# An encoder layer on one core: the order of VectorE and ScalarE in attention written out, pv copied whole by ScalarE, its halves added by GpSimd, and o stored in two parts

## The chip, the core and the metric

The kernel runs on one core of one Trainium2 chip. The metric is device time in microseconds: the median of several executions. "The profiled execution" is one of them, taken with the hardware profiler; all durations of single instructions come from it. In the profile PE is TensorE (PEld its weight loads), DVE VectorE, ACT ScalarE, POOL GpSimd and SP SyncE; a q behind a name is that engine's instruction queue.

## The reference, cut to what matters

One layer with two token mixers over 1024 prompt frames and 64 frames of a running stream (1088 columns together). The part that the change touches is the band attention, and the gates and merge behind it:

```python
s = einsum('bqhd,bkhd->bhqk', q, k) * HEAD_DIM ** -0.5
s = where(allowed, s + bias, NEG_INF)   # own chunk of 64 and the 8 chunks before
p = softmax(s)
o = einsum('bhqk,bkhd->bqhd', p, v)     # 8 heads of 64
yb = o @ w_attn_out
merged = sigmoid(ga) * ya + sigmoid(gb) * yb
```

Ahead of it stand a norm and the combined input projection; behind it an output projection, a gated feed-forward part and two norms. All is 32-bit; the kernel gets its precision by splitting each operand into a rounded high part (hi) and the rest (lo), and taking products of the parts.

## The kernel before

**Attention** is a list of 72 tiles: 8 heads, and in each 9 tiles t (eight of 128 prompt frames, t = 0 to 7; t = 8 is the 64 frames of the stream with its cache). A loop in `attention` (line 974 on) walks over this list in steps, and a step i does the following for tiles at different distances:

- `scores` of tile i: the S products (q times k) into a PSUM bank of kind "att"; then `softmax`: VectorE adds the bias and takes the maximum (L856), ScalarE takes the exp with its row sums (L866);
- `transposed` of tile i - 2: TensorE turns p into a PSUM bank "att" (T, L774); then `split`: ScalarE casts it to hi (L122), VectorE subtracts to get lo (L123);
- `values` of tile i - 4, for odd t (two tiles together) and t = 8: the pv products into the one bank "pv". With hi and lo of v as 128 weight columns, pv has two halves of 64 rows, and hi and lo of p make two halves of its columns. `combine` adds all: ScalarE copies the lower 64 rows (L872), VectorE adds the upper 64 (L873), GpSimd adds the two column halves (L874), and SP's queue stores the result into o_d (L877, L881). For t = 8, the reciprocals of the row sums are turned too, copied by ScalarE (L949) and stored by GpSimd's queue in four parts (L951, L955).
- between these, `gate` hands out products of the gates ga and gb (32 pieces of 24 products; 5 run before attention, 16 in it, 11 after). A finished piece lies in the bank "mm" during attention, ScalarE copies it out (L792) and GpSimd's queue stores it (L793). After a piece is finished, the next call of `gate` gives nothing.

The banks are "att" 3, "mm" 1, "pv" 1. TensorE's order is the program's: `mm_at` and `turned` pin each product and turn. The order on ScalarE, VectorE, GpSimd and in SP's queue is set at compile time by a planner that takes, among the instructions that its own clock holds ready, the first of the program.

`head_load` (from line 822) loads q, k, bias and v of a head through SP's queue one head ahead; q, k, v have two buffers, the stream's keys and values (ks, vs) one.

**The merge** (from line 1014): SP's queue loads the gates of the first block (L1002), u (L1017), and for each quarter k of the 512 rows of o the rows of o_d (L1020) and the reciprocal sums, spread over 64 rows a head (L1024, tile rc with two buffers). VectorE multiplies (L1027), and `split` makes the hi and lo parts ob. Then the last gate pieces are handed out, and block by block TensorE takes ya (from u) and yb (from ob), L302, and VectorE multiplies each with its gate (L1043, L1048).

Of the kernel before, what the change touches and what calls it, by code (L numbers as in the profile page):

```python
# [65 lines left out]
def encoder_kernel(ctx: ExitStack, tc: tile.TileContext, ins, outs):  # L66
# [701 lines left out]
    mm0, turned0 = nc.tensor.matmul, nc.tensor.transpose  # L768

    def mm_at(*a, **kw):  # L770
        tc.keep_in_program_order(mm0(*a, **kw))  # L771

    def turned(*a):
        tc.keep_in_program_order(turned0(*a))  # L774

    def gates():

        kinds = itertools.chain(["att"] * (4 * len(GATES) - WITH - BEHIND), ["mm"] * WITH, turns)
        pieces = [(i, c) for cs in ((0, 1), (2, 3)) for i in range(2) for c in cs]
        pieces += [(i, c) for i in range(2, len(GATES)) for c in range(4)]  # L780
        w = {}
        for i, c in pieces:
            g, m = GATES[i]
            o, n = PIECES[c]
            if i not in w:
                w[i] = next_w()
# [5 lines left out]
            act.copy(st[:, :n], ps[:, :n])  # L792
            nc.gpsimd.dma_start((ga_d if g == "a" else gb_d)[m * P : (m + 1) * P, o : o + n], st[:, :n])  # L793
            yield True

    turns = itertools.cycle(["mm", "pv", "att", "att", "att"])
# [3 lines left out]
    def gate(upto, stop=True):  # L800


        if given[1]:
            given[1] = False
            return
        while given[0] < upto:
            given[0] += 1
            if next(gate_products) and stop:
                given[1] = True
                break  # L810

    heads, sums = {}, {}

# [38 lines left out]
    def softmax(s, ps, bias, sm, nm):  # L852

        rows = s.shape[0]
        mx = at_pool.tile([P, 1], F32, tag="mx", name=f"mx{nm}", bufs=3)[:rows]
        vec.tensor_tensor_reduce(  # L856
            out=s.rearrange("p (a b) -> p a b", a=ps.shape[1]),
            in0=ps,
            in1=bias.rearrange("p (a b) -> p a b", a=ps.shape[1]),
            scale=-1.0,  # L860
            scalar=3e38,
            op0=ALU.add,
            op1=ALU.min,
            accum_out=mx,
        )
        act.activation(s, s, AF.Exp, bias=mx, scale=-1.0, accum_out=sm)  # L866

    def combine(h, pv, n, tok, nm):

        a = at_pool.tile([HD, 2, 256], F32, tag="cmb_a", name=f"ca{nm}", bufs=1)  # L870
        o = at_pool.tile([HD, 256], F32, tag="cmb_o", name=f"co{nm}", bufs=3)
        act.copy(a[:, :, :n], pv[HD:])  # L872
        vec.tensor_tensor(a[:, :, :n], pv[:HD], a[:, :, :n], op=ALU.add)  # L873
        pool_e.tensor_tensor(o[:, :n], a[:, 0, :n], a[:, 1, :n], op=ALU.add)  # L874
        if tok < TP:
            c = tok if tok < 512 else HT + tok - 512
            nc.sync.dma_start(o_d[h * HD : (h + 1) * HD, c : c + n], o[:, :n])  # L877
        else:
            for e in range(2):
                c = 512 + e * HT  # L880
                nc.sync.dma_start(o_d[h * HD : (h + 1) * HD, c : c + 32], o[:, 32 * e : 32 * e + 32])  # L881

    def scores(h, t):
        q, k, ks, v, vs, bias = heads[h]
        ps = bank("att", f"s{h}_{t}")
        s = at_pool.tile([P, 640], F32, tag="s", name=f"p{h}_{t}", bufs=4)
        if t < 8:
            nb = min(t + 1, 5)
            k0, n, r = (t - nb + 1) * P, nb * P, P
            q0 = t * P if t < 4 else t * P + TS  # L890
        else:
            k, k0, n, r = ks, 0, CACHE + TS, TS
            q0 = 512
# [12 lines left out]
        softmax(s[:r, :n], ps, bias[:r, b0 : b0 + n], sm[:r, t : t + 1], f"{h}_{t}")  # L906
        return s

    pts = {}

    def transposed(h, t, s):
        tp = bank("att", f"t{h}_{t}")
        if t == 8:
            pt = at_pool.tile([P, 2, 5, TS], F32R, tag="pts", name=f"pts{h}", bufs=1)
            for i in range(4):
                turned(
                    tp[:, i * TS : (i + 1) * TS], s[:TS, i * P : (i + 1) * P], ident[:TS, :TS]
                )
            turned(tp[:TS, 4 * TS : 5 * TS], s[:TS, 512:576], ident[:TS, :TS])
            split(pt[:, 0, :4, :], pt[:, 1, :4, :], tp[:, : 4 * TS].rearrange("p (b t) -> p b t", t=TS))  # L920
            split(pt[:TS, 0, 4, :], pt[:TS, 1, 4, :], tp[:TS, 4 * TS : 5 * TS])
            pts[h, 4] = pt

            vec.reciprocal(sums[h], sums[h])
# [11 lines left out]
        split(pt[:, 0, b0 : b0 + nb, js], pt[:, 1, b0 : b0 + nb, js], src)  # L936

    def values(h, t):
        q, k, ks, v, vs, bias = heads[h]
        pv = bank("pv", f"pv{h}_{t}").rearrange("p (a b) -> p a b", a=2)  # L940
        if t == 8:
            pt = pts.pop((h, 4))
            for i in range(5):
                r = P if i < 4 else TS
                mm_at(pv[:, :, :TS], vs[:r, i, :], pt[:r, :, i, :], start=i == 0, stop=i == 4)
            tr = pv[:9, 1, P:]
            turned(tr, sums.pop(h), ident)
            rows = at_pool.tile([P, P], F32, tag="rows", name=f"rows{h}", bufs=1)[:9]
            act.copy(rows, tr)  # L949
            for e in range(2):  # L950
                nc.gpsimd.dma_start(  # L951
                    rc_d[h, e * HT : e * HT + 512].rearrange("(t p) -> t p", p=P), rows[4 * e : 4 * e + 4]
                )
                c = e * HT + 512
                nc.gpsimd.dma_start(rc_d[h : h + 1, c : c + 32], rows[8:9, 32 * e : 32 * e + 32])  # L955
            combine(h, pv[:, :, :TS], TS, TP, f"{h}_s")
            return
        g = t // 2
# [15 lines left out]
    def attention():  # L974
        order = [(h, t) for h in range(NH) for t in range(9)]
        done = []
        n = len(order)

        share = [3] * 2 + [1] * (n - 2) + [3] * 4
        upto = [24 * WITH * v // sum(share) for v in itertools.accumulate(share)]  # L980
        first = given[0]
        for i in range(n + 4):
            if i < n:
                h, t = order[i]
                if t == 3 and h + 1 < NH:
                    head_load(h + 1)
                done.append(scores(h, t))
            gate((given[0] + first + upto[i]) // 2)
            if i >= 4:
                h, t = order[i - 4]  # L990
                if t % 2 or t == 8:
                    values(h, t)
            if 0 <= i - 2 < n:
                transposed(*order[i - 2], done[i - 2])
            gate(first + upto[i])

    def gates_in(m):
        sg = {}
# [17 lines left out]
    for k in range(4):  # L1016
        nc.sync.dma_start(u.t[:, :, k].bitcast(F32), u_d[k])  # L1017
    for k in range(4):
        o = ob.t[:, 0, k].bitcast(F32)
        nc.sync.dma_start(o, o_d[k * P : (k + 1) * P])  # L1020
        r = mp.tile([P, T], F32, tag="rc", name=f"rc{k}", bufs=2)
        for j in range(2):
            src = rc_d[2 * k + j]
            nc.sync.dma_start(  # L1024
                r[j * HD : (j + 1) * HD], bass.AP(tensor=src.tensor, offset=src.offset, ap=[[0, HD], [1, T]])
            )
        vec.tensor_tensor(r, o, r, op=ALU.mult)  # L1027
        split(ob.t[:, 0, k], ob.t[:, 1, k], r)
    all_of(gate_products)


    mg = quarters("mg")
# [582 lines left out]
```

## Time and profile before

| | |
|---|---|
| median of 3 runs | 1539.54 us (1539.33 to 1543.82) |
| profiled execution | 1537.84 us, span 1535.7 us, mean granted clock 0.989 |
| busy, share of the span | PE 96%, DVE 64%, ACT 45%, POOL 10% |
| attention | about 397 to 577 us of the span |
| last gate pieces and start of the merge | about 577 to 630 us |

How to read it: the span is first to last instruction of the profiled execution; the time has some 2 us around it. A wait is given as engine, line, releaser, total us, times, longest. In rows of groups, the columns are line, engine, operation, out<-in, shapes and count, then busy us and mean ns of one, then idle us ahead of them with the releasers. In the timeline the first two columns are start and duration in us, and brackets hold the idle time before and its releaser. The granted clock is a share of full speed.

### The profile page before, as it was taken

To read this page: it belongs to the slowest core of one execution; us is meant where nothing else is said; L and a number is where in the kernel's file an instruction comes from. 1 tells how busy PE (TensorE), PEld (TensorE's weight loads), DVE (VectorE), ACT (ScalarE), POOL (GpSimd) and SP (SyncE) were. 2 spreads that over 40 slices of the span, in tenths; PEclk is the share of its full clock that TensorE was granted. 3 is DMA by queue.
4 is the path that set the end of the run, shared out by engine and by line. 5 is a ranking of instruction groups with operands and counts; after the bars stand their busy time and mean duration, and the time that the engine had idled before them with its cause. 6 is when DMAs were issued, how large, how long until landed. Compare 5 with 4: busy or idle time off the path is not lost.

```text
span 1535.7 us, 26422 instructions
## 1 busy us (share of the span) xinstructions
PE 1477.0 (96%) x10130; PEld 1380.8 (90%) x10130; DVE 983.5 (64%) x1823; ACT 685.1 (45%) x1395; POOL 146.7 (10%) x260
## 2 busy tenths in 40 slices
PE   7999999999888899999999999999999999999997
PEld 5799999999877789998888999999999998788886
DVE  6886465464466661664279766666666668857576
ACT  6654333333576672453156444444444445503123
POOL 1210010000133322000000010000010111000000
PEclk9999999999999999999999999999999999999999
DMA  7597623225866648654332443333443449666675
GB/s 236 180 303 232 199 68 130 77 85 195 217 177 163 158 117 260 192 156 152 134 130 75 150 155 128 135 122 125 152 154 141 155 151 308 236 236 230 219 261 199
DMA packets 167903, 264.74 MB, mean 172 GB/s; under 512 B 18880, under 2 KB 103040, under 8 KB 167648
## 3 DMA queue, kind: packets, MB, share of 16 engines
q1 hardware_dynamic: 147888, 200.46, 41.7%
q0 software_dynamic: 18736, 60.49, 10.8%
q10 hardware_dynamic: 1152, 2.10, 0.4%
q8 instruction: 80, 1.31, 0.4%
q14 instruction: 47, 0.39, 0.1%
HBM read 171.06 MB, written 91.92 MB: 171 GB/s over the span
## 4 chain that ended last, share of the span: by engine, by line
PE 62%; issue 24%; DMA 4%; DVE 4%; ACT 3%; POOL 2%; SPq 1%; POOLq 0%; ACTq 0%; DVEq 0%
PE A L1532 7%; PE Ab L239 6%; PE Aa L239 6%; PE D L1532 3%; PE Db L239 3%; PE Da L239 3%; PE g L771 2%; PE pv L771 2%; PE B L1532 2%; PE s L771 2%; PE Ak L239 2%; PE Bb L239 2%; PE Acc L239 2%; PE Acb L239 2%; PE Agb L239 2%
## 5 line engine op out<-in xcount | busy, mean ns | idle before, releaser
L1532 PE MATMUL A<-ring,ht 128*128 128x512 f32 x528 | 128.4, 398 | 1.4 <-DVE acc L1544 1.1
L1532 PEld LDWEIGHTS A<-ring,ht 128*128 128x128 f32 x528 | 100.3, 191 | 25.4 <-DVE acc L1544 1.8
L771 PE MATMUL g<-xn,whp 128*128 128x272 f32 x512 | 113.6, 303 | 5.7 <-ACT gst L792 4.7
L771 PEld LDWEIGHTS g<-xn,whp 128*128 128x128 f32 x512 | 84.9, 193 | 9.0 <-ACT gst L792 6.7
L122 ACT CAST ring<-w2r 128x512 fp32r<-128x512 f32 (+1 forms) x78 | 43.6, 587 | 106.6 <-PE A L1532 53.6
L122 ACT CAST hq<-sa 128x512 fp32r<-128x512 f32 x77 | 47.7, 619 | 85.1 <-DVE sa L1263 56.8
L1251 POOL DMA_DIRECT2D h_d<-hq x77 | 41.1, 533 | 416.9 <-DVE hq L123 239.7
L771 PE MATMUL g<-xn,wlp 128*128 128x272 f32 x256 | 76.8, 300 | 0.0
L123 DVE TENSOR_TENSOR hq<-sa,hq 128x512 fp32r<-128x512 f32 x77 | 53.2, 690 | 32.2 <-ACT hq L122 32.0
L1532 PE MATMUL D<-ring,ht 128*128 128x512 f32 x264 | 64.5, 396 | 1.9 <-ACT acc L1542 1.9
L123 DVE TENSOR_TENSOR wla<-rawa,wha 128x512 fp32r<-128x512 f32 x56 | 38.5, 688 | 40.5 <-ACT wha L122 40.5
L1532 PEld LDWEIGHTS D<-ring,ht 128*128 128x128 f32 x264 | 49.8, 189 | 13.7 <-ACT acc L1542 2.3
L239 PE MATMUL Aa<-tt,wha 128*128 128x272 f32 x352 | 59.2, 289 | 2.8 <-ACT tt L122 2.5
L239 PE MATMUL Ab<-mg,whb 128*128 128x272 f32 x352 | 58.4, 288 | 0.0
L239 PE MATMUL Aa<-mg,wha 128*128 128x272 f32 x352 | 58.3, 288 | 0.0
L239 PE MATMUL Ab<-tt,whb 128*128 128x272 f32 x352 | 58.2, 287 | 0.0
L123 DVE TENSOR_TENSOR ring<-w2r,ring 128x512 fp32r<-128x512 f32 (+1 forms) x78 | 49.2, 647 | 13.5 <-ACT ring L122 13.2
L122 ACT CAST wha<-rawa 128x512 fp32r<-128x512 f32 x56 | 34.8, 621 | 50.9 <-PE Ab L239 35.0
L866 ACT ACTIVATE p<-p,mx 128x640 f32<-128x640 f32 (+5 forms) x72 | 50.9, 707 | 12.4 <-DVE mx L856 11.8
L302 PE MATMUL yb<-ob,whp 128*128 128x272 f32 x256 | 50.5, 294 | 2.6 <-ACT ob L122 1.9
L239 PEld LDWEIGHTS Aa<-tt,wha 128*128 128x128 f32 x352 | 49.8, 189 | 3.5 <-ACT tt L122 2.9
L1544 DVE TENSOR_TENSOR acc<-A,acc 128x512 f32<-128x512 f32 x52 | 35.7, 687 | 26.5 <-PE A L1532 26.4
(539 smaller groups left out, 4312.3 us busy)
## 6 DMA issues: line engine op xcount, KB each, us to landing
h_d<-hq POOLq DMA_DIRECT2D x77, 512.0 KB, 3.5
ht<-h_d SPq DMA_DIRECT2D x154, 256.0 KB, 3.5
rawa<-in_w_ff SPq DMA_DIRECT2D x11, 1024.0 KB, 5.6
rawb<-in_w_ff SPq DMA_DIRECT2D x11, 1024.0 KB, 5.3
w2r<-in_w_ff SPq DMA_DIRECT2D x11, 1024.0 KB, 6.2
qd<-q_d SPq DMA_DIRECT2D x32, 272.0 KB, 5.2
u_d<-scr SPq DMA_DIRECT2D x8, 544.0 KB, 4.2
ga<-ga_d SPq DMA_DIRECT2D x32, 136.0 KB, 2.2
```

The lines of the kernel that those rows point to most:

```text
L122: act.copy(hi, src)
L123: vec.tensor_tensor(lo, src, hi.bitcast(F32), op=ALU.subtract)
L239: mm(t[:, j, :HN], w[:, k, :], x[p][:, l, k, j * HN : (j + 1) * HN], start=p in (1, 2, 7) and k == 0 and n == 0, stop=k == 3 and n == 2, s ...
L302: mm(out, l, r, start=k + j == 0, stop=k == kt - 1 and j == 2)
L771: tc.keep_in_program_order(mm0(*a, **kw))
L866: act.activation(s, s, AF.Exp, bias=mx, scale=-1.0, accum_out=sm)
L1251: nc.gpsimd.dma_start(h_d[p, c - 1], hq.rearrange("p i l t -> p (i l t)").bitcast(F32))
L1532: mm(t, ht[k][:, j, x], w[:, l], start=p in (1, 2, 7) and k == 0 and n == 0, stop=k == len(ks) - 1 and n == 2, skip_group_check=p in (6, 5 ...
L1544: vec.tensor_tensor(o, t, o, op=ALU.add)
```

## The change

In `attention`, every instruction of TensorE, VectorE and ScalarE gets an edge from the one pinned before it on its engine (`pin`, an edge for the planner, without a semaphore). What follows a product is no longer issued with it: it goes into lists by kind (`todo`), and each step takes the lists at fixed places (`take`). In a step the order is: first part of the gate products; S of tile i; then the gate copy, the casts of the tile turned in the step before, the copies of finished pv, the reciprocal, the subtractions; T of tile i - 2; pv of tile i - 4 (odd t) or i - 5 (t = 8); the rest of the gate products; the exp of tile i - 1; the maximum of tile i. The loop has 77 steps where it had 76. GpSimd and the DMA queues are not pinned.

`combine` now has ScalarE copy all 128 rows of pv, and GpSimd add the two column halves of all 128 rows; the two halves of rows are stored apart, into o_d of twice the size, through GpSimd's queue. Merge: each quarter loads both parts (r and o2), VectorE adds them (new), then multiplies with the reciprocal sums. r has two buffers; o2 and the sums are loaded into the places of ob's lo and hi. The gate pieces are copied by VectorE instead of ScalarE.

```diff
-    o_d = dr.tile([ATT, T], F32, name="o_d")
+    o_d = dr.tile([2, ATT, T], F32, name="o_d")
...
+    newest = {}
+    def pin(i):
+        i = i.ins
+        if i.engine in newest:
+            why = mybir.DependencyInfo(mybir.DependencyClass.NoSync, mybir.DependencyReason.DATA)
+            tc.add_manual_dep(i, newest[i.engine], why, reason="order of the steps")
+        newest[i.engine] = i.name
+    def pinned(f):
+        return lambda *a, **kw: pin(f(*a, **kw))
+    mm_at, turned = pinned(nc.tensor.matmul), pinned(nc.tensor.transpose)
+    max_at, tt_at, inv_at = pinned(vec.tensor_tensor_reduce), pinned(vec.tensor_tensor), pinned(vec.reciprocal)
+    exp_at, copy_at = pinned(act.activation), pinned(act.copy)
+    tt_copy = pinned(vec.tensor_copy)
+    todo = {kind: [] for kind in "max exp hi lo inv o gate".split()}
+    def take(kind):
+        for f in todo[kind]:
+            f()
+        todo[kind].clear()
...
-            st = st_pool.tile([P, HN], F32, tag="st", name=f"gst{i}_{c}")
-            act.copy(st[:, :n], ps[:, :n])
-            nc.gpsimd.dma_start((ga_d if g == "a" else gb_d)[m * P : (m + 1) * P, o : o + n], st[:, :n])
+            def out(ps=ps, nm=f"gst{i}_{c}", dst=(ga_d if g == "a" else gb_d)[m * P : (m + 1) * P, o : o + n], n=n):
+                st = st_pool.tile([P, HN], F32, tag="st", name=nm)
+                tt_copy(st[:, :n], ps[:, :n])
+                nc.gpsimd.dma_start(dst, st[:, :n])
+            todo["gate"].append(out)
...
     def combine(h, pv, n, tok, nm):
-        a = at_pool.tile([HD, 2, 256], F32, tag="cmb_a", name=f"ca{nm}", bufs=1)
-        o = at_pool.tile([HD, 256], F32, tag="cmb_o", name=f"co{nm}", bufs=3)
-        act.copy(a[:, :, :n], pv[HD:])
-        vec.tensor_tensor(a[:, :, :n], pv[:HD], a[:, :, :n], op=ALU.add)
-        pool_e.tensor_tensor(o[:, :n], a[:, 0, :n], a[:, 1, :n], op=ALU.add)
...
+        def f():
+            a = at_pool.tile([P, 2, 256], F32, tag="a", name=f"ca{nm}", bufs=1)
+            o = at_pool.tile([P, 256], F32, tag="o", name=f"co{nm}", bufs=3)
+            copy_at(a[:, :, :n], pv)
+            pool_e.tensor_tensor(o[:, :n], a[:, 0, :n], a[:, 1, :n], op=ALU.add)
+            to = o_d[:, h * HD : (h + 1) * HD]
...
+            for c, e, w in spans:
+                nc.gpsimd.dma_start(to[:, :, c : c + w], o[:, e : e + w])
+        todo["o"].append(f)
...
-        for i in range(n + 4):
+        for i in range(n + 5):
+            target = first + upto[min(i, n + 3)]
+            gate((given[0] + target) // 2)
             if i < n:
                 h, t = order[i]
                 if t == 3 and h + 1 < NH:
                     head_load(h + 1)
                 done.append(scores(h, t))
-            gate((given[0] + first + upto[i]) // 2)
-            if i >= 4:
-                h, t = order[i - 4]
-                if t % 2 or t == 8:
-                    values(h, t)
+            for kind in ("gate", "hi", "o", "inv", "lo"):
+                take(kind)
             if 0 <= i - 2 < n:
                 transposed(*order[i - 2], done[i - 2])
-            gate(first + upto[i])
+            for lag, kinds in ((4, (1, 3, 5, 7)), (5, (8,))):
+                if 0 <= i - lag < n and order[i - lag][1] in kinds:
+                    values(*order[i - lag])
+            gate(target)
+            take("exp")
+            take("max")
+        take("o")
+        take("gate")
...
     for k in range(4):
-        o = ob.t[:, 0, k].bitcast(F32)
-        nc.sync.dma_start(o, o_d[k * P : (k + 1) * P])
-        r = mp.tile([P, T], F32, tag="rc", name=f"rc{k}", bufs=2)
+        rc, o2 = (ob.t[:, l, k].bitcast(F32) for l in range(2))
+        r = mp.tile([P, T], F32, tag="rc", name=f"r{k}", bufs=2)
+        nc.sync.dma_start(r, o_d[0, k * P : (k + 1) * P])
+        nc.sync.dma_start(o2, o_d[1, k * P : (k + 1) * P])
...
-        vec.tensor_tensor(r, o, r, op=ALU.mult)
+        vec.tensor_tensor(r, r, o2, op=ALU.add)
+        vec.tensor_tensor(r, r, rc, op=ALU.mult)
         split(ob.t[:, 0, k], ob.t[:, 1, k], r)
-    all_of(gate_products)
+    gate(24 * 4 * len(GATES), False)
```

In the same way the maximum and the exp, the casts and subtractions of T, the reciprocal and the copy of the turned sums go into the lists "max", "exp", "hi", "lo", "inv" and "o".

More of the change, by code (lines that the diff above doesn't have):

```diff
@@ L807, in gate @@
             given[0] += 1
-            if next(gate_products) and stop:
-                given[1] = True
-                break
+            if next(gate_products):
+                if stop:
+                    given[1] = True
+                    break
+                take("gate")
     heads, sums = {}, {}
@@ L948, in values, with out @@
             rows = at_pool.tile([P, P], F32, tag="rows", name=f"rows{h}", bufs=1)[:9]
[L949 to L955, printed above, removed]
+            def out():
+                copy_at(rows, tr)
+                for e in range(2):
+                    nc.gpsimd.dma_start(
+                        rc_d[h, e * HT : e * HT + 512].rearrange("(t p) -> t p", p=P), rows[4 * e : 4 * e + 4]
+                    )
+                    c = e * HT + 512
+                    nc.gpsimd.dma_start(rc_d[h : h + 1, c : c + 32], rows[8:9, 32 * e : 32 * e + 32])
+            todo["o"].append(out)
             combine(h, pv[:, :, :TS], TS, TP, f"{h}_s")
@@ L987, in attention @@
                 done.append(scores(h, t))
[L988 to L992 removed]
+            for kind in ("gate", "hi", "o", "inv", "lo"):
+                take(kind)
             if 0 <= i - 2 < n:
                 transposed(*order[i - 2], done[i - 2])
[L995 removed]
+            for lag, kinds in ((4, (1, 3, 5, 7)), (5, (8,))):
[5 more added lines that the diff above has]
+        take("o")
+        take("gate")
     def gates_in(m):
```

59 lines of the change are left out of this document (27 added, 32 removed).

## The prediction, made before the changed kernel was run

> **What bounds the kernel now.** I read the page first, then busy time by windows of the attention stage (397 to 577 us), then the waits of TensorE in it, then the timeline at one of them.
>
> ```profile
> span 1535.7 us, 26422 instructions
> PE 1477.0 (96%) x10130; PEld 1380.8 (90%) x10130; DVE 983.5 (64%) x1823; ACT 685.1 (45%) x1395; POOL 146.7 (10%) x260
> ```
>
> Over the whole span TensorE is busy, so only stages in which it pauses can give time. Attention is one (columns: window, length, then busy us and count of PE, PEld, DVE, ACT, POOL, granted clock, DMA share, GB/s):
>
> ```profile
> 397.00:577.00 180.00, 159.14 (x1080) 145.25 (x1080) 120.74 (x282) 126.18 (x298) 49.76 (x85) 0.97 0.62 158
> 443.00:450.00 7.00, 4.18 (x31) 3.85 (x30) 3.28 (x8) 3.20 (x8) 2.83 (x6) 1.00 0.41 120
> 485.00:495.00 10.00, 7.18 (x42) 6.57 (x41) 4.33 (x10) 4.60 (x13) 3.60 (x7) 0.83 0.50 112
> 530.00:540.00 10.00, 7.64 (x46) 7.48 (x47) 4.59 (x11) 4.80 (x12) 3.99 (x8) 0.83 0.64 158
> ```
>
> In 180 us TensorE stands for 180 - 159.14 = 20.9 us, and no other engine is full: per step of the 72 it has 159.14/72 = 2.2 us, ScalarE 1.75, VectorE 1.68, GpSimd 0.69. So this is a stage of waits and not of an engine's throughput. The waits, in the form engine, line, releaser, us in total, times, longest:
>
> ```profile
> PE pv L771 <- issue: 12.3, 6, 3.1
> PE g L771 <- ACT gst L792: 4.2, 8, 0.8
> PE pv L771 <- DVE pt L123: 0.8, 3, 0.4
> PE t L774 <- DVE mx L856: 0.5, 2, 0.3
> PE s L771 <- DVE pt L123: 0.5, 1, 0.5
> PE pv L771 <- DVE ca L873: 0.4, 1, 0.4
> ```
>
> The largest has no releaser by name ("issue"). The timeline at one of the six names it:
>
> ```profile
> 486.94 0.72 ACT L866 ACTIVATE p<-p,mx 128x512 f32<-128x512 f32 x1 [1.20 <-DVE mx L856]
> 487.78 0.58 ACT L872 COPY ca<-pv 64x512 f32<-64x512 f32 x1
> 488.40 0.68 DVE L873 TENSOR_TENSOR ca<-pv,ca 64x512 f32<-64x512 f32 x1 [1.55 <-ACT ca L872]
> 489.18 1.26 PE L771 MATMUL pv<-pts,vsd 128*128 128x128 f32 x5 [2.82 <-issue]
> ```
>
> The streaming tile's pv products (t = 8) need the one pv bank that t = 7 has just filled. ScalarE's queue has an exp ahead of the copy out of that bank; the exp waits 1.20 us for VectorE's maximum; then come the copy and VectorE's add, and TensorE starts 0.1 us after that add ends. It is a queue order, once a head.
>
> **Part one: the order and the copy of pv.** In the new loop each step emits, on ScalarE: casts of the T of the step before, the copy of a finished pv, exp of the scores of the step before; on VectorE: the gate copy, the subtraction, the maximum of this step. So the copy of t = 7's pv stands ahead of that exp by construction, no VectorE add is in the path, and the t = 8 products come two steps after t = 7's instead of one. Between them lies more than a step, 2.2 us, against one copy. The costs:
>
> ```profile
> L866 ACT ACTIVATE p<-p,mx 128x640 f32<-128x640 f32 (+5 forms) x72 | 50.9, 707 | 12.4 <-DVE mx L856 11.8
> L856 DVE CUSTOM_DVE_ANT_0 p<-s,bb 128x640 f32<-128x640 f32 (+5 forms) x72 | 47.5, 661 | 5.1 <-PE s L771 3.9 <-DMA bb<-bias_d 0.3 <-DMA ksd<-k_d 0.3
> L123 DVE TENSOR_TENSOR pt<-t,pt 128x640 fp32r<-128x640 f32 (+2 forms) x64 | 41.8, 655 | 12.9 <-ACT pt L122 10.4
> L122 ACT CAST pt<-t 128x640 fp32r<-128x640 f32 (+2 forms) x64 | 35.7, 560 | 10.5 <-PE t L774 9.4
> L873 DVE TENSOR_TENSOR ca<-pv,ca 64x512 f32<-64x512 f32 x32 | 21.8, 682 | 19.8 <-ACT ca L872 19.8
> 437.56 0.71 PE L774 MATMUL t<-ident,p 128*128 128x128 f32 x5
> L874 POOL TENSOR_TENSOR co<-ca 64x256 f32<-64x256 f32 x32 | 23.7, 739 | 84.4 <-DVE ca L873 70.5 <-DMA o_d<-co_s 8.2 <-DMA kd<-k_d 5.6
> L951 POOL DMA_DIRECT2D rc_d<-rows x15 | 7.9, 523 | 8.6 <-ACT ca_s L872 8.6
> L792 ACT COPY gst<-g 128x272 f32<-128x272 f32 x15 | 5.7, 383 | 0.4 <-PE g L771 0.4
> ```
>
> - Pauses at the pv bank: -12.3 us.
> - TensorE's waits for the gate copy: -4.2 us. The copy becomes the first VectorE instruction of the next step, and the loop skips a gate turn after a finished piece, so it has half a step to get done. Bounds 0 and -4.2; I take all of it, since VectorE is the less loaded: it loses 21.8 us of adds and gains 15 copies x 0.38 = 5.7 us (not shown on VectorE; nearest row, ScalarE's).
> - The clock. In 485 to 495 and 530 to 540 the mean clock is 0.83, a loss of 0.17 x 10 = 1.7 us each, behind pauses of 2.8 and 3.1 us: -3.4 us. [...]
> - The small waits on pt, mx and ca (0.8 + 0.5 + 0.5 + 0.4 = 2.2): the pins can mend or worsen them; I take half, -1.1 (bounds -2.2 and +2.2).
> - Does the strict order close a loop that is longer than TensorE's step? From T of one step to T three steps on, the chain is T 0.71 (a row of the timeline), cast 0.56, subtraction 0.66, maximum 0.66, exp 0.71: 3.3 us over three steps, 1.1 a step against 2.2. It doesn't.
> - New waits. The tile for the copied pv has one buffer, so ScalarE's copy of the next pv waits until GpSimd has added the halves of the last. After t = 8, GpSimd first issues four row stores (0.52 each, 2.1 us) and only then adds. The next copy is due one step later, 2.2 us after the rows: a tie. Bounds 0 and one add, 0.74 us, a head: 0 to +6; I take the middle, +3.
> - One more step in the loop (77 for 76): ahead of the last pv products stands the second half of a step's gate products, which covers the one copy, 0.
> - The o stores move from SP's queue to GpSimd's: 48 issues x 0.52 = 25 us more on an engine with 49.8 of 180, behind no one's path but the next add's (priced above). SP's queue loses them: 0, as TensorE's waits don't name SP now.
>
> Attention: -12.3 - 4.2 - 3.4 - 1.1 + 3 = **-18.0 us**.
>
> **Part two: the merge.** Now, in time (start, duration):
>
> ```profile
> 575.98 0.26 ACT L872 COPY ca_s<-pv 64x128 f32<-64x128 f32 x1
> 580.10 0.34 SPq L1002 DMA_DIRECT2D ga<-ga_d  x1
> 608.60 1.29 DVE L1027 TENSOR_TENSOR rc<-ob,rc 128x1088 f32<-128x1088 f32 x1 [18.94 <-DMA rc<-rc_d]
> 612.38 1.09 SPq L1024 DMA_DIRECT2D rc<-rc_d  x2
> 618.66 1.28 DVE L1027 TENSOR_TENSOR rc<-ob,rc 128x1088 f32<-128x1088 f32 x1
> 621.12 0.39 PE L302 MATMUL yb<-ob,whp 128*128 128x272 f32 x1 [1.91 <-ACT ob L122]
> ```
>
> The loads are the limit: the first quarter's data land at 608.6, TensorE finds the third quarter of ob late and stands 1.91 us. The loads' size and pace:
>
> ```profile
> ob<-o_d SPq DMA_DIRECT2D x4, 544.0 KB, 17.2
> 590.00:600.00 10.00, 10.00 (x82) 10.00 (x81) 0.00 (x0) 1.16 (x3) 1.63 (x3) 1.00 1.00 405
> 600.00:605.00 5.00, 5.00 (x42) 5.00 (x41) 0.00 (x0) 0.39 (x1) 0.54 (x1) 1.00 1.04 254
> ```
>
> Each quarter now loads a second 544 KB and has one more VectorE addition of 1.29 us. For the first two quarters, which start together, that is two loads more, and one less, since the third quarter's now waits: 0.56 MB at 405 to 254 GB/s, 1.4 to 2.2 us. The third quarter must wait for the first one's buffer (as its row factors do now, at 612.38), but with both its o loads behind that wait: 1.11 MB, 2.8 to 4.4 us. Two additions stand in its path, 2.6 us. Together 6.8 to 9.2 us later. Against that: SP's first load of the merge (580.10) stands behind the last o stores; with these gone it can start up to 580.1 - 576.2 = 3.9 us sooner; and TensorE can be given the next block's ya products meanwhile, 48 of them at 10/82 = 0.122 us, 5.9 us. So the ends are 6.8 - 3.9 - 5.9 = -3.0 and +9.2; nothing here says which the compiler's order takes, so the middle: **+3 us**. After it TensorE is the bound again and the additions cost nothing.
>
> **Sum.** -18 + 3 = -15 us on the profiled execution, 1537.84 us (its span and 2.1 us around it): 1522.8. The median of the runs, 1539.54, is 1.7 above that execution, so 1524.5.
>
> **Rivals.**
>
> *GpSimd holds ScalarE (slower).* Nothing pins GpSimd's queue: a gate store that stands ahead of an addition while its data are late holds the addition, then ScalarE's next copy, and with it the casts and exps behind. The trace has it once:
>
> ```profile
> 529.60 0.56 POOL L793 DMA_DIRECT2D ga_d<-gst  x1 [7.77 <-ACT gst L792]
> 530.96 0.58 ACT L872 COPY ca<-pv 64x512 f32<-64x512 f32 x1 [1.65 <-POOL co L874]
> ```
>
> Here GpSimd stood 7.77 us for a gate copy and ScalarE 1.65 us for GpSimd. With VectorE making the gate copies late in its queue, the 16 gate stores of the stage would each cost it: 16 x 1.65 = 26.4, with the -21 of the other terms and +3 of the merge +8: 1548. It decides from 18/16 = 1.1 us a store on. Against it: the gate copy leads VectorE's step. 0.12.
>
> *The loads come late.* SP waits for the t = 8 products before it refills their values, and the keys of two heads on come behind that:
>
> ```profile
> SPq L848 <- PE pv L774: 18.2, 7, 4.0
> 450.01 1.23 SPq L836 DMA_DIRECT2D kd<-k_d  x2
> kd<-k_d SPq DMA_DIRECT2D x32, 128.0 KB, 5.6
> 458.56 0.44 PE L771 MATMUL s<-kd,qd 128*128 128x128 f32 x2 [0.51 <-DVE pt L123]
> ```
>
> The first keys land at 451.2 + 5.6 = 456.8 and are used at 458.56: 1.8 us to spare. The t = 8 products come a step (2.2 us) later and one o store less (0.5) stands between, so the spare is about 0.1, and less as heads get shorter by 18/8 = 2.3 us. The most: 7 heads x 2.2 = 15 us, which takes the whole gain back; half of it gives 1532. Against it: with the o stores gone SP reaches the free loads sooner. 0.14, half of it faster by over 0.3%.
>
> *The pins repeat the order that stands already:* attention the same, the merge +3: 1542.5. Against it: the timeline shows the exp ahead of the copy, which the new order turns round. 0.06.
>
> *The merge takes its worst* (+9.2) and the small waits and GpSimd's tie theirs (+2.2, +6): -12.3 - 4.2 - 3.4 + 2.2 + 6 + 9.2 = -2.5: 1537. 0.08.
>
> **How the numbers follow.** Forecast 0.60, 1524.5 us. Its best end: -12.3 - 4.2 - 3.4 - 2.2 - 3.0 = -25: 1514.5; 2 us are left for stalls inside the busy time that no row prices: 1512. The range ends at 1540, above the late loads and the worst merge, and leaves out GpSimd's hold and part of the unchanged order. A measurement of this kernel can tell about 0.3%, 4.6 us. Faster by more: 0.60 + 0.07 = 0.67; within: half of the late loads (0.07), the worst merge (0.08) and half of the unchanged order (0.03) = 0.18; slower: 0.12 + 0.03 = 0.15.
>
> **What would show it.** Right: "issue" ahead of pv gone from TensorE's waits, the attention stage near 162 us, the clock 1.00 in it; ScalarE's copy of pv starting within 0.3 us of its last product; TensorE's wait for ob near 5 us in the merge. Wrong: ScalarE's copies waiting for GpSimd's addition; S products waiting for k or q; VectorE standing for a gate store in the merge while ob is due.

## The result and the profile after

The changed kernel takes 1537.6 us in the median of 20 runs, against 1537.9 us of the kernel before in 20 runs on the same chips: ratio 0.9996, 95% interval 0.998 to 1.0012. The forecast was 1524.5 us. The two kernels can't be told apart. One of the 20 runs of the kernel before took 5200 us; a median hardly feels it.

The page of the profiled execution after, its first lines:

```profile
span 1536.7 us, 26391 instructions
...
PE 1476.1 (96%) x10130; PEld 1380.4 (90%) x10130; DVE 976.6 (64%) x1819; ACT 668.7 (44%) x1363; POOL 186.7 (12%) x308
```

The stages are cut at three points that can be read in every trace: the first S product, the stream's last pv product, the last yb product. Busy time by windows of the kernel after: the two stages, then three stretches of the merge (columns as in the prediction):

```profile
395.90:565.00 169.10, 155.33 (x1073) 143.10 (x1073) 102.97 (x258) 116.03 (x281) 87.34 (x129) 0.96 0.81 185
565.00:710.80 145.80, 135.94 (x1034) 133.71 (x1034) 80.85 (x179) 53.91 (x135) 10.67 (x19) 0.95 0.63 191
605.00:615.00 10.00, 6.86 (x32) 5.90 (x32) 8.37 (x11) 2.20 (x2) 0.65 (x2) 0.68 0.67 198
615.00:625.00 10.00, 4.40 (x28) 3.74 (x28) 5.39 (x6) 2.50 (x3) 0.00 (x0) 0.84 0.89 271
625.00:635.00 10.00, 9.95 (x64) 9.63 (x65) 8.90 (x22) 5.49 (x15) 0.00 (x0) 0.80 0.51 154
```

The same two stages of the kernel before:

```profile
575.10:712.10 137.00, 133.87 (x1046) 132.69 (x1046) 72.45 (x166) 58.64 (x148) 9.04 (x18) 0.99 0.62 190
397.20:575.10 177.90, 157.24 (x1066) 143.46 (x1066) 120.46 (x281) 125.66 (x296) 48.60 (x83) 0.97 0.62 159
```

So attention became 177.9 - 169.1 = 8.8 us shorter and the merge 145.8 - 137.0 = 8.8 us longer. What lies behind went from 823.6 to 825.9 us and what lies ahead from 397.2 to 395.9, both untouched by the change; over the runs below the last stage scatters from 821 to 828, and what lies ahead from 396 to 401. The spans differ by 1.0 us. The question is why attention gave 8.8 and not 18, and why the merge took 8.8 and not 3.

**Attention.** The waits of TensorE in it, and three rows of other engines from the same view:

```profile
PE s L779 <- DMA kd<-k_d: 8.9, 6, 1.9
PE t L779 <- DVE mx L779: 2.7, 2, 2.3
...
SPq L872 <- PE pv L779: 13.0, 4, 6.1
...
DVE p L779 <- DMA bb<-bias_d: 16.2, 6, 5.7
...
ACT ca L779 <- POOL co_s L883: 6.2, 7, 1.8
```

"issue" ahead of pv and the wait for the gate copy are gone, as forecast. In their place TensorE waits for the keys and VectorE for the bias of the next head (in the kernel before, one wait of 2.8 us for keys and 0.3 for bias). In both kernels one of the waits for keys belongs to the very first S product and ends where the stage begins (2.8 us before, 1.9 after). So between the heads TensorE waited for keys not once before, and 7.0 us in 5 waits after. ScalarE does wait for GpSimd's addition of the stream's part, 0.9 us a head, but none of TensorE's waits names it. The timeline at a head boundary of the kernel after:

```profile
424.39 0.36 SPq L872 DMA_DIRECT2D vsd<-v_d  x1
427.17 2.52 SPq L860 DMA_DIRECT2D kd<-k_d  x4
431.08 0.45 SPq L864 DMA_DIRECT2D bb<-bias_d  x1
435.00 0.42 PE L779 MATMUL s<-kd,qd 128*128 128x128 f32 x2 [1.88 <-DMA kd<-k_d]
440.48 0.48 PE L779 MATMUL t<-ident,p 64*128 64x64 f32 x5 [2.33 <-DVE mx L779]
...
436.00:446.00 10.00, 7.67 (x42) 6.61 (x42) 2.85 (x12) 4.20 (x12) 1.98 (x3) 0.83 0.86 219
```

SP's queue is let go by the stream's pv products (first row), then asks for q, the keys and the bias. The S products of the next head stand 1.88 us for the keys, T 2.33 us for a maximum that had waited 5.71 us for the bias, and the clock is 0.83 (last row, a window), after 1.00 in the 10 us ahead of it. From the release of the queue to the moment at which S was due, the kernel after leaves 435.00 - 1.88 - 424.39 = 8.7 us; the kernel before left 10.9 at the boundary that the prediction shows (S at 458.56 after a wait of 0.51, the queue's release at 447.12, below). Over the six boundaries that can be read this way it is 8.1 to 8.7 us after and 10.6 to 12.8 before.

```profile
447.12 0.36 SPq L848 DMA_DIRECT2D vsd<-v_d  x1
```

**The merge.** TensorE's waits in it, then SP's and VectorE's, then three rows on the quarters (minimum, median and maximum in ns, first to last start in us):

```profile
PE yb L302 <- ACT ob L122: 6.2, 4, 3.6
PE yb L302 <- DVE ob L123: 1.5, 2, 0.9
...
SPq L1064 <- DVE ob L123: 22.6, 2, 18.7
...
SPq L1064 <- DMA o_d<-co_s: 6.0, 1, 6.0
...
DVE gst L779 <- DMA gb_d<-gst: 29.0, 8, 5.0
...
L1064 SPq DMA_DIRECT2D r<-o_d x4: 325/326/1142, 577.3 to 613.9; - x4
...
L122 ACT CAST ob<-r x4: 1097/1099/1102, 605.5 to 623.6; 128x1088 fp32r<-128x1088 f32 x4
```

The rows on the quarters before (here o is loaded into ob's place):

```profile
L1020 SPq DMA_DIRECT2D ob<-o_d x4: 325/584/891, 586.8 to 613.5; - x4
...
L122 ACT CAST ob<-rc x4: 1098/1100/1105, 609.9 to 624.7; 128x1088 fp32r<-128x1088 f32 x4
```

Counted from the end of attention, the last quarter is cast 623.6 - 565.0 = 58.6 us later, before 624.7 - 575.1 = 49.6. TensorE stands 145.8 - 135.9 = 9.9 us in the stage (before 3.1), and the clock is 0.68, 0.84 and 0.80 in three windows in a row.

### The profile page after: what moved, and what is told of

Same layout as the page of the kernel before. It is cut to its first block, busy times and chain, and to the rows that moved or that the text cites. A ratio compares the mean times of both kernels' runs of the same rounds, so it can differ in the third digit from the quotient of the medians.

```text
span 1536.7 us, 26391 instructions
## 1 busy us (share of the span) xinstructions
PE 1476.1 (96%) x10130; PEld 1380.4 (90%) x10130; DVE 976.6 (64%) x1819; ACT 668.7 (44%) x1363; POOL 186.7 (12%) x308
## 4 chain that ended last, share of the span: by engine, by line
PE 62%; issue 19%; DMA 11%; DVE 4%; ACT 2%; POOL 1%; SPq 0%; POOLq 0%; ACTq 0%; DVEq 0%
PE Ab L239 7%; PE Aa L239 7%; PE A L1577 7%; PE Db L239 4%; PE Da L239 4%; PE D L1577 3%; PE Bb L239 2%; PE B L1577 2%; PE g L779 2%; PE Ak L239 2%; DMA kd<-k_d 2%; PE Ba L239 2%; PE Acc L239 2%; PE Ach L239 2%; PE Acb L239 2%
## 5 line engine op out<-in xcount | busy, mean ns | idle before, releaser
L779 PE MATMUL g<-xn,whp 128*128 128x272 f32 x512 | 105.7, 297 | 1.0 <-ACT scr L531 1.0
L779 DVE CUSTOM_DVE_ANT_0 p<-s,bb 128x640 f32<-128x640 f32 (+5 forms) x72 | 47.9, 665 | 40.1 <-PE s L779 20.4
L1577 PEld LDWEIGHTS D<-ring,ht 128*128 128x128 f32 x264 | 49.5, 188 | 14.2 <-ACT acc L1587 2.8
L239 PEld LDWEIGHTS Aa<-tt,wha 128*128 128x128 f32 x352 | 49.6, 188 | 4.7 <-ACT tt L122 2.9
```

Source lines behind the costliest of these rows:

```text
L239: mm(t[:, j, :HN], w[:, k, :], x[p][:, l, k, j * HN : (j + 1) * HN], start=p in (1, 2, 7) and k == 0 and n == 0, stop=k == 3 and n == 2, s ...
L779: return lambda *a, **kw: pin(f(*a, **kw))
L1577: mm(t, ht[k][:, j, x], w[:, l], start=p in (1, 2, 7) and k == 0 and n == 0, stop=k == len(ks) - 1 and n == 2, skip_group_check=p in (6, 5 ...
```

## The experiments

All kernels start from the changed one, except where it is said. Ratios are to the kernel before, run on the same chip. The stages, cut as above, from each profiled execution (us; stall is the stage less TensorE's busy time):

| kernel | ratio, 95% | attention, stall, clock | merge, stall, clock |
|---|---|---|---|
| before | 1 | 177.9, 20.7, 0.97 | 137.0, 3.1, 0.99 |
| the changed kernel | 0.9996 (0.998 to 1.0012) | 169.1, 13.8, 0.96 | 145.8, 9.9, 0.95 |
| e1_tail_act | 0.9971 (0.9953 to 0.999) | 162.9, 12.3, 0.99 | 142.4, 8.8, 0.98 |
| e2_vs_late | 0.9982 (0.9965 to 0.9998) | 164.0, 11.9, 0.98 | 144.8, 9.2, 0.96 |
| e3_o_one | 0.9939 (0.9919 to 0.9958) | 171.1, 14.2, 0.99 | 134.5, 3.0, 0.99 |
| e4_all_three | 0.9938 (0.9916 to 0.996) | 171.6, 14.5, 0.99 | 133.8, 2.5, 0.99 |
| e5_loads | 0.9915 (0.9897 to 0.9932) | 157.8, 6.8, 0.99 | 146.0, 9.1, 0.95 |
| e6_best | 0.9848 (0.9832 to 0.9864) | 157.8, 6.3, 0.99 | 135.2, 3.7, 0.99 |
| e7_no_pin | 0.9992 (0.9976 to 1.0008) | 163.1, 13.7, 1.00 | 145.9, 9.8, 0.95 |
| e8_o_two | 0.9951 (0.9932 to 0.9971) | 166.3, 11.2, 0.98 | 145.8, 10.5, 0.96 |
| e9_lag4 | 0.9958 (0.9942 to 0.9974) | 166.2, 13.9, 0.97 | 146.4, 9.4, 0.95 |
| e10_no_add | 0.998 (0.996 to 1.0) | 164.7, 13.8, 0.99 | 145.0, 10.2, 0.95 |
| e11_no_load | 0.9927 (0.9901 to 0.9953) | 167.7, 12.4, 0.96 | 139.0, 7.3, 1.00 |
| e12_loads_act | 0.987 (0.9847 to 0.9892) | 153.8, 4.0, 0.99 | 145.3, 10.8, 0.95 |

A single profile scatters: the attention of after, e1, e10 and e11 is the same code and lasted 169.1, 162.9, 164.7 and 167.7 us, at a clock of 0.96, 0.99, 0.99 and 0.96 and with TensorE busy for 155.3, 150.6, 151.0 and 155.3 us. So attention's time is sure to some 6 us, its gain by these four over the one profile of the kernel before lies between 8.8 and 15.0, and verdicts rest on the ratios and on stalls with a name. The merge scatters less: the same code took 144.8 to 146.4 us in after, e2, e5 and e9.

### Where the merge's time went

**e1_tail_act**: the gate pieces behind attention copied by ScalarE, not pinned.

```diff
-                tt_copy(st[:, :n], ps[:, :n])
+                (act.copy if attended else tt_copy)(st[:, :n], ps[:, :n])
```

> The changed kernel, but the gate pieces that are handed out after attention are copied by ScalarE, unpinned, as before. Theory A (VectorE's pinned gate copies, which wait 29 us for the stores of earlier pieces, keep the merge's first addition until 602.6 us, though its loads were issued at 577 to 583): the first addition starts by 595, TensorE's waits for ob in the merge fall from 7.7 us to under 3, and the time falls by 5 to 9 us against the changed kernel. Theory B (the merge is late because each quarter has two o loads, one more addition and a buffer to wait for): quarters still come 6 us apart, TensorE's waits stay over 5 us, and the time moves by less than 3 us.

1533.4 us, between the two theories: 3.8 us less by the ratios, whose intervals overlap. The merge is 3.4 us shorter in the profile (the fastest of the twelve executions, 1526.3 us), with 8.8 of the 9.9 us of stall still there. VectorE's waits for gate stores (29.0 us above) are a small part of the merge's loss at most.

**e3_o_one**: the pinned order kept, but pv added by VectorE as before (pinned), o stored in one part through GpSimd's queue, and the merge of the kernel before.

```diff
-            a = at_pool.tile([P, 2, 256], F32, tag="a", name=f"ca{nm}", bufs=1)
-            copy_at(a[:, :, :n], pv)
+            a = at_pool.tile([HD, 2, 256], F32, tag="a", name=f"ca{nm}", bufs=1)
+            copy_at(a[:, :, :n], pv[HD:])
+            tt_at(a[:, :, :n], pv[:HD], a[:, :, :n], op=ALU.add)
...
```

> The changed kernel with its pinned order, but pv is added as before (ScalarE copies the lower rows, VectorE adds the upper ones, now pinned behind the subtractions), o is stored in one part, by GpSimd's queue, and the merge has neither the second loads nor the additions. Theory B: the merge's quarters come 5 us apart or less, TensorE's waits for ob fall under 3 us, total -6 to -9 us. Theory A: the gate copies still hold the first quarter until 602, TensorE still waits some 4 us for it, total -2 to -4 us. Attention: the pause at the pv bank stays away in both (the end of the stream's pv products within 2 us of 565).

1527.8 us. The merge's loss is gone to the last: 134.5 us, 3.0 us of stall. Attention is not shorter than in the kernel after (171.1 us), and the pauses at the pv bank stay away though VectorE's addition is back. But the addition brings other waits, in TensorE's waits of this kernel:

```profile
PE s L779 <- DVE pt L779: 9.2, 18, 1.4
```

**e10_no_add** and **e11_no_load** take the two costs of o in two parts one by one: e10 leaves out the addition `vec.tensor_tensor(r, r, o2, op=ALU.add)`, e11 the load of o2 (r is added to itself).

> The changed kernel without VectorE's addition of the two parts of o in the merge (left out of the computation; both parts are still loaded). Theory (the second loads and the two buffers of r set the merge): the quarters still come some 6 us apart, the merge stays at 144 to 146 us, the time within 2 us of 1537.6. Rival (the additions set it): two additions of 1.3 us lie in the path of the third quarter and each gate copy waits less, so the merge falls by 2.6 us or more, to 143 or less, and the time to 1535 or less.

> The changed kernel without the loads of the second part of o in the merge (left out; VectorE adds the first part to itself instead, so the number of additions and the two buffers of r stay). Theory (the second loads cost the time): the merge falls from 145.8 to about 138 us and the time by 6 to 8 us, to about 1530.5 (0.995). Rival (the two buffers of r, behind which the third and fourth quarter's loads stand, cost it, whatever is loaded): the merge falls by less than 3 us, and the time stays at 1535 or above.

e10: 1534.5 us, its interval overlapping that of after; the merge 145.0, the stall 10.2. e11: 1528.9 us, the merge 139.0. The casts of the quarters in e10 (first row) and e11 (second row; attention ends at 561.0 and 564.2), and a window of e11:

```profile
L122 ACT CAST ob<-r x4: 1097/1097/1105, 598.9 to 618.5; 128x1088 fp32r<-128x1088 f32 x4
```

```profile
L122 ACT CAST ob<-r x4: 1097/1099/1110, 599.9 to 615.8; 128x1088 fp32r<-128x1088 f32 x4
...
604.20:614.20 10.00, 6.61 (x45) 5.75 (x45) 7.46 (x9) 2.20 (x2) 0.00 (x0) 1.00 0.99 259
```

The last quarter comes 57.5 us after attention without the additions and 51.6 without the second loads, against 58.6 in the kernel after and 49.6 before. So of 9.0 us the second loads cost 7.0 and the additions 1.1. The merge of after stands in e2, e5 and e9 too, and there it is 57.9 to 58.8: the price of the loads is far outside of this scatter, that of the additions hardly. That r's two buffers make the later quarters wait (SP's 22.6 us above) costs little by itself: e11 keeps them, and of the 2.0 us by which its last quarter comes later than before (51.6 against 49.6) the additions take 1.1.

### Where attention's gain went

**e7_no_pin**: the new order without the pins of VectorE and ScalarE (`if i.engine in newest and i.engine == mybir.EngineType.PE`).

> The changed kernel without the pins of VectorE and ScalarE: the program's order and the two-part o stay, TensorE's order is the same, and the planner is free to set the two engines' order; in attention it puts an exp ahead of the copy of pv in many steps. If the pins bring attention's gain, the pauses at the pv bank come back and the stream's last pv products start at 570 to 575 us; if the new places in the program and the missing addition bring it, they start within 3 us of 565 and the total is that of the changed kernel.

1536.1 us, as after. The waits for keys stay (10.2 us, 5 times). The pins by themselves give and cost nothing that can be measured, to within some 3.5 us.

**e8_o_two**: the other way round: the kernel before, with only the whole copy of pv, GpSimd's addition, the store in two parts and the new merge; the order is the planner's, the gate copies ScalarE's.

> The kernel before with one part of the change alone: pv copied whole by ScalarE, halves added by GpSimd, o stored in two parts by GpSimd's queue, added in the merge; order and gate copies as before. Theory B (o in two parts makes the merge some 11 us longer): from the stream's last pv products to the last yb 143 to 148 us instead of 137, TensorE's waits for ob over 7 us; attention gains at most the 0.7 us of the addition at each of 8 pauses; total +3 to +8 us over the kernel before. Rival (only together with the pinned gate copies does the merge get longer): total within 2 us.

1529.2 us: a gain where a loss was expected. The merge costs as much as after (145.8), but attention gained 11.6 us without the new order. Its timeline at a head boundary:

```profile
442.66 0.62 ACT L866 ACTIVATE p<-p,mx 128x384 f32<-128x384 f32 x1 [0.30 <-DVE mx L856]
443.49 0.59 ACT L872 COPY ca<-pv 128x512 f32<-128x512 f32 x1
444.44 0.81 PE L771 MATMUL pv<-pts,vsd 128*128 128x128 f32 x5
445.20 0.72 ACT L866 ACTIVATE p<-p,mx 128x512 f32<-128x512 f32 x1 [0.96 <-DVE mx L856]
```

The pv products start without a stall, 0.4 us after the copy. The exp of 384 columns ahead of the copy is not the one that made the pause in the prediction's timeline: that was the next, of 512 columns, and here it comes behind the copy (last row), at every head that has one. So the planner's own order changed with the addition gone, and e8 can't tell the order from the addition. The six pauses of the kernel before can, and they are of three kinds. In two (2.8 us each) the exp of 512 columns stands ahead of the copy, as the prediction has it. In three (1.2 us each) the copy is in time, and VectorE's addition comes behind a maximum:

```profile
465.17 0.58 ACT L872 COPY ca<-pv 64x512 f32<-64x512 f32 x1
465.80 0.69 DVE L856 CUSTOM_DVE_ANT_0 p<-s,bb 128x512 f32<-128x512 f32 x1 [0.34 <-PE s L771]
466.42 0.68 DVE L873 TENSOR_TENSOR ca<-pv,ca 64x512 f32<-64x512 f32 x1
467.20 0.89 PE L771 MATMUL pv<-pts,vsd 128*128 128x128 f32 x5 [1.18 <-issue]
```

In one (3.1 us) the copy waits 1.65 us for GpSimd, in the lines of the prediction's first rival. Either half of the change removes all of them: the new order with the addition kept (e3), or the addition taken out with the planner's order (e8). TensorE's wait for the gate copy stayed here (4.3 us, 7 times).

**e2_vs_late** and **e5_loads** move loads. e2 puts only the stream's values (vs), the load that holds SP's queue, behind the next head's loads, at t = 6. e5 spreads them: q, k, bias and v of the next head at t = 3, the stream's keys (ks) at t = 0 and its values at t = 5 of their own head.

```diff
+                if t == 0 and h:
+                    stream_keys(h)
+                if t == 5 and h:
+                    stream_values(h)
...
```

> The changed kernel, but the stream's values of a head are loaded three steps later in the program, so that SP's queue no longer waits for the t = 8 products ahead of the next but one head's q, k and bias. Theory C (in attention, 8 to 10 us of the gain are lost to keys and bias that land late: TensorE waits 8.9 us for k, VectorE 16.2 us for the bias): these waits fall under 2 us, the last pv products of the stream start at 557 to 559 us instead of 565. Rival: the loads are late because the transfers themselves are slow (DMA share 0.8 to 0.9), and the waits stay. The total falls by 5 to 8 us if the merge moves along with attention, and by less than 2 if the merge takes it back as it did with the first gain.

> The changed kernel, with a head's loads spread over the steps: q, k, bias and v of the next head at t = 3, the stream's values at t = 5 of their own head (behind the products that free their buffer), the stream's keys at t = 0. Neither stands ahead of the next head's k in SP's queue while it waits. Theory C (late loads cost attention its missing gain): neither k nor the stream's values are waited for (under 2 us together, after 8.9 for k before and 9.6 for values in the run that loaded these late); last pv products of the stream at 555 to 558 us, and the total 4 to 8 us under the changed kernel's. Rival (the transfers are too many for the shorter heads): a wait for some load of 5 us or more stays.

e2: 1535.6 us; no wait for keys is left, but a new one has come, TensorE's for vs: in the program vs now stands behind ks, whose load needs the S products of t = 8 done (SP's queue waits 5.8 us, 3 times, for S products at that load in the kernel after; that it does so in e2 is the author's estimate). e5: 1524.4 us. TensorE's first wait in attention in e2, then in e5:

```profile
PE pv L779 <- DMA vsd<-v_d: 9.6, 6, 2.5
```

```profile
PE pv L779 <- DMA vsd<-v_d: 3.7, 3, 1.6
```

From after to e5 the ratio falls by 0.0081, 12.5 us (some 9 to 16 by the two intervals); attention falls from 169.1 to 157.8 and the stall by half. That is the price of the late loads. The clock, 0.99 here, is no part of it that is shown: e1, e7 and e10 have the waits for keys (8.5, 10.2 and 9.9 us) and 0.99 to 1.00 as well.

**e9_lag4**: the t = 8 products four steps after their S products, as before the change (`((4, (1, 3, 5, 7, 8)),)`).

> The changed kernel, but the stream's pv products (t = 8) again four steps after their S products instead of five, in the new fixed order. Theory (the later step is what makes the loads late): the queue's wait for these products ends a step, 2.2 us, sooner, so the keys and the bias of the next head but one come in time: TensorE's wait for kd falls from 7.0 us (5 times) below 2, VectorE's for bb from 16.2 below 8, and the time by 4 to 6 us, to about 1532 (ratio 0.996). Rival (the loads are late because the heads got shorter, whatever the step): the wait for kd stays at 5 us or more, and the time within 2 us of 1537.6. Either way no wait at the pv bank should come back, because the copy of t = 7 still stands ahead of the exp in ScalarE's order.

1532.8 us: the time of the theory, but not its mechanism. The waits in attention and SP's at the boundary:

```profile
PE s L779 <- DMA kd<-k_d: 7.1, 6, 2.2
...
440.21 0.37 SPq L872 DMA_DIRECT2D vsd<-v_d  x1
...
452.31 0.42 PE L779 MATMUL s<-kd,qd 128*128 128x128 f32 x2 [2.21 <-DMA kd<-k_d]
```

The wait for keys has not gone, nor that for bias (16.6 us). S of the next head was due at 452.31 - 2.21 = 450.1, 9.9 us after the release of SP's queue: 1.2 us more than in the kernel after, 1.0 less than before. Over six boundaries it is 9.7 to 10.4. So the later step took about half of the time that was lost between the kernel before and after, the shorter head the rest, and giving back the one half wasn't enough. At this boundary part of it was lost in SP's queue again, which asked for the keys 3.6 us after its release, against 2.8 in the kernel after. Which stall gave the 5 us is open: the profiled execution's stall is the same (13.9 us).

### The edits together

**e4_all_three** is e3 with e1's and e2's edits. **e12_loads_act** is after with e5's and e1's, o in two parts. **e6_best** is e12 with o in one part as in e3, and VectorE's addition of pv pinned at the end of the step's copies and subtractions, so that it no longer stands ahead of a subtraction:

```diff
-            for kind in ("gate", "hi", "o", "inv", "lo"):
+            for kind in ("gate", "hi", "o", "inv", "lo", "add"):
```

> All three edits together: pinned order in attention, ScalarE's copies of the gate pieces behind attention, o in one part, the stream's values loaded late. If attention's gain of 10 us was lost in the merge, and 7 more are lost to the late loads: attention's end at 558, TensorE's waits in the merge as before the change (2.5 us), total 1537.6 - 10 - 7 = 1520 (1516 to 1525). If the merge is bound by its loads whatever is done ahead of it, under 5 us of this are seen: over 1532.

> The changed kernel with two edits that were run alone before: the loads of the next head spread over the steps (alone 0.9915), and the gate copies behind attention by ScalarE, unpinned (alone 0.9971). O in two parts stays. If they cost in different places, they add: 1537.6 - 13.2 - 4.2 = 1520.2 us (0.9886), with attention at 158 us and the merge at 142. What is left to the best kernel (1512.2), 8 us, is then the price of o in two parts alone. If the second hides in the first: 1523 to 1524, and o in two parts costs 11.

> The pinned order with o in one part, spread loads, ScalarE's copies of the gate pieces behind attention, and VectorE's addition of pv's halves of rows pinned behind the subtractions of its step instead of ahead of them. If the waits of S for the subtraction (9.2 us in the run with one part) come from the addition standing ahead of it, these fall under 3 us and the end of the stream's pv products comes to 560 to 564 us (571 there); with the merge's 134 us from there to its last yb, as in the runs with one part, the total is 1518 to 1523. If VectorE is simply too full with the addition, the waits stay and the total is that of the one-part run, 1527.

e4: 1527.3 us, nothing more than e3, where 1520 was expected. The 9.2 us of waits behind VectorE's addition are all there; that they hide what the other two edits give is not shown. e12: 1519.6 us, as expected in sum, but not in its parts: attention was 153.8 (158 expected, the code of e5) and the merge 145.3 (142 expected), so ScalarE's gate copies did not shorten the merge here. Nor are VectorE's needed for its loss: e8, with ScalarE's copies throughout, has 145.8. Against e5 the ratio is 0.0045 lower, 6.9 us, with intervals that don't touch. So the edit does gain, but the profiles show the gain only in stages that it leaves as they were, and where it comes from stays open. e6: 1512.2 us, ratio 0.9848, faster than both kernels and than the 1518 to 1523 expected. The waits of S for a subtraction are gone. It differs from e4 in two edits, the spread loads and the addition's place, and what each gave is not separated. Its two stages:

```profile
396.00:553.80 157.80, 151.54 (x1073) 138.85 (x1073) 122.95 (x297) 118.74 (x281) 73.92 (x129) 0.99 0.71 183
553.80:689.00 135.20, 131.53 (x1034) 130.78 (x1033) 74.12 (x170) 58.94 (x148) 10.01 (x19) 0.99 0.62 189
```

With o in two parts (e12) attention is 4.0 us shorter and the merge 10.1 longer. The two intervals (0.9847 to 0.9892 and 0.9832 to 0.9864) overlap a little, so that o in one part wins is likely, not sure; it is sure without the spread loads (e3 against after).

## Why the prediction was wrong

- **Pauses at the pv bank, -12.3:** right in size; the "issue" row is gone. The reason was read at one of the six pauses and taken for all. "It is a queue order, once a head" holds for ScalarE's queue at two of them (5.6 us); at three it was VectorE's addition behind a maximum (3.5 us), at one GpSimd (3.1 us). That the change removed all of them is partly luck: it took the addition out too.
- **Waits for the gate copy, -4.2:** right, none left in attention. e8, with ScalarE's copies, keeps them (4.3 us).
- **The clock, -3.4:** not shown either way. It is 0.96 after against 0.97 before, one profile each, and the same attention code had 0.96 to 0.99 in four.
- **Small waits, -1.1:** not borne out; the waits for maxima alone are 2.7 us after, against 2.2 for all that the prediction counted, and 2.3 of them follow the late bias.
- **GpSimd's tie, +3:** it is there on ScalarE (6.2 us, 7 times), and TensorE names it nowhere: nothing of it is seen in the time.
- **The rival "loads come late", 0.14:** this is the first step that failed. The prediction had the mechanism, the row (1.8 us to spare) and a ceiling of 15 us, then set it aside because "with the o stores gone SP reaches the free loads sooner". But the load that holds the queue is not a free one: it waits for the t = 8 products. e5 puts the price at 11 to 12.5 us. Without it attention is 177.9 - 157.8 = 20.1 us shorter (24.1 in e12), so that the -18 were near the truth for an attention whose loads come in time.
- **The merge, +3, bounds -3.0 and +9.2:** the second step that failed. The loads and additions together were sized well, 6.8 to 9.2 forecast and 9.0 measured for the last quarter, but the parts were not: 4.2 to 6.6 for the loads, which cost 7.0, and 2.6 for the additions, which cost about 1. That the sum fits is luck. The two credits were hardly there. SP did start sooner: the gates of the first block, asked for from 580.1 on before, were all asked for by 565.4. But the first o load (577.3) came no sooner after attention's end, 12.3 us, against 11.7 before (586.8), since it waits 6.0 us for the o stores, which now stand on GpSimd's queue. And the ya products covered little: TensorE's stall in the stage grew by 6.8 us, from 3.1 to 9.9, and its busy time by 2.1, at a clock of 0.95 against 0.99. The middle between two far ends was taken without a row for the credits; +8.8 came.
- **Sum:** -20.1 (attention) + 11.3 (late loads) + 8.8 (merge) = 0.0, with +2.3 and -1.3 outside of the two stages the 1.0 us between the spans. The terms are of single profiles and sure to some 6 us; the sum, by the ratio, to some 2.5. The result lies inside the range (1512 to 1540), but by two cases together that the prediction had kept apart, the late loads and the merge near its worst; to a time that can't be told from before it had given 0.18.
- **The signs named in advance** did answer: S products waiting for k was listed as a sign of being wrong, and it is TensorE's first wait. VectorE standing for gate stores was listed too and came (29.0 us), but e12 moves those copies to ScalarE, and the merge stays as long. Of the signs of being right, "issue" is gone; the attention stage near 162 us and the wait for ob near 5 us came out at 169.1 and 7.7 us in the kernel after.
- **The pins** were neither the gain nor the loss (e7).

## What to carry to other kernels

When a stage gets faster, read how far ahead of their use its loads land, and subtract the expected gain from that spare before the gain is booked: here SP's queue asked for the keys 2.8 us after the stream's pv products had let it go, and TensorE waited for keys for 7.0 us between the heads. A step that moves a consumer later can move the loads behind its buffer, too: here the time from the release of the queue to S grew by 1.2 us when the t = 8 products stood one step earlier again (e9). And an addition taken out of a tight loop by storing two parts was paid here where the parts are read again, with 9.0 us at the last quarter, 7.0 of them for the second loads; a credit that is to hide that price needs a row of its own. And a pause that comes six times is read six times: one of them may not stand for the rest.

## What the hardware showed that was not expected

A lower clock came with some of TensorE's pauses and not with others, and their length didn't tell which. In the kernel after the clock was 0.83 in the window with pauses of 1.88 us (ending 1 us ahead of it) and 2.33 us (attention), and 0.68, 0.84 and 0.80 in the merge's three windows, with a longest wait of 3.6 us. In the kernel before it was 0.83 in the window 485 to 495 and 1.00 in 443 to 450, with a pause of 2.82 us in each. And in e11 it stayed 1.00 across a window with 3.4 us of stall, none of its waits longer than 2.3 us:

```profile
PE yb L302 <- ACT ob L122: 3.7, 2, 2.3
```

What in a pause decides it wasn't settled. Single profiles of one and the same attention differ by up to 6.2 us, 4.8 of them in TensorE's busy time (155.33 us at 0.96, 150.55 at 0.99), which is as much as some of the edits are worth.
